# The end of a mixture-of-experts layer: expert 15's product ahead of expert 14's sums, parts taken straight from the accumulators, another split of the last LayerNorm

## Chip, core and metric

The kernel runs on one core of a Trainium2 chip. The metric is device microseconds of one execution. TensorE is written PE in the profile, VectorE DVE, ScalarE ACT, GpSimd POOL, SyncE SP; PSUM is the memory in which PE sums, SBUF the working memory.

## What is computed

One decoder layer on 512 tokens of width 1024. Only its last stage matters here: 16 experts, of which every token uses two, and a LayerNorm over the sum.

```python
for e in range(N_EXPERTS):                       # 16
    hidden = jax.nn.silu(hf @ w1[e]) * (hf @ w3[e])          # 1024 -> 512
    y = y + combine[:, e:e + 1] * (hidden @ w2[e])           # 512 -> 1024
...
h = layer_norm(DN_ALPHA * h + moe_out, ln3_g[l], ln3_b[l])
```

## The kernel before

Each expert has a block of 128 slots; its tokens are gathered into them from memory. `up(e)` makes the hidden rows, `turn_hidden(e)` transposes them on PE (four transposes, then one DVE copy, line L1453), `down(e)` makes the second product. Both products have a base part, which does slots 0 to 63 with matmuls 64 rows high, and a further part in `further`, which PE enters by a branch on the expert's token count: slots 64 to 95 if it has over 64 tokens, 96 to 127 if it has over 96. `down` sums the base part in the PSUM tile `a` (I-5387_acc in the rows; its two halves of partitions hold the two halves of the columns) and the further part in the PSUM tile `b` (I-5389_acc; four groups of 32 partitions, which hold the four quarters of the columns, with slots 64 to 95 in columns 0:256 and slots 96 to 127 in 256:512). There is one `a` and one `b` for all experts.

After `down(e)` ACT and DVE move the sums out and scale them by the tokens' gates: `a` in two ACT instructions of 64x512, `b` in four ACT and four DVE instructions of 32x256. For experts 0 to 13 the rows go to SBUF and a POOL DMA adds them into `yd` in memory, which already holds the residual. The program makes ACT and DVE wait for each other wherever both read the tile `b`, whichever partitions they read.

Experts 14 and 15 don't go through memory. Their scaled rows are split into a high part of 32-bit "r" type and a low rest (`split`, L191 on ACT and L192 on DVE), and for each of the four tiles of 128 tokens PE multiplies a 0/1 matrix `own[e]` by both parts (`combine`, L1535 and L1536: four matmuls of 128x512 per tile and expert). The tile's rows from `yd` are added either by PE with an identity (`from_memory`, L1557, tiles 0 and 2) or by DVE while it takes the sums (`totals`, L1573, tiles 1 and 3). The last LayerNorm then goes tile by tile: the sums (`sums_vector` for tile 0, `totals` and `mean` for the others), the squares on ACT (`deviation`, L1582) with two small POOL instructions behind them (L1583 and the power -1/2, L214), the centred rows times the gain on DVE (`centred`, L1589, L1592), and the scaling with the shift: on DVE (`shifted`, L1602), or on ACT with an addition on POOL (`scaled`, L1596 and L1597: tile 0 and half of tile 1). SP sends the rows out.

Each engine works through its own list in the order of the program; a semaphore lets an instruction wait for another engine. The order of the end is written out by hand:

```python
    h = up(NE - 1)
    r = last_loads()
    load_tiles(range(NT))
    parts(NE - 2, down(NE - 2), r)
    turn_hidden(NE - 1, h)
    begin_tile(0)                       # expert 14's part of tiles 0 and 1
    begin_tile(1)
    parts(NE - 1, down(NE - 1), 3)
```

Of the kernel before, what the change touches and what calls it, by code (L numbers as in the profile page):

```python
# [96 lines left out]
def tile_kernel(ctx, tc, x, mem, ln_in_g, ln_in_b, w_in, hg_lb_logits, hg_norm_g, w_branch_a, w_branch_b,  # L97
# [1357 lines left out]

    def down(e):
        x, (a, b) = hT.pop(e), sums_down
        ws = [W.get(j) for j in q_w2[e]]
        for k, w in enumerate(ws):
            for n in range(2):  # L1460
                nc.tensor.matmul(a[64 * n:64 * n + 64], x[:, k, 0:64], w[:, n * 512:(n + 1) * 512], start=k == 0,  # L1461
                                 stop=k == 3)
            tick()
# [12 lines left out]
        y = ys[e % 2]  # L1476
        for n in range(2):
            s = slice(64 * n, 64 * n + 64)
            nc.scalar.activation(y[0:64, n * 512:(n + 1) * 512], a[s], AF.Copy, scale=gates_at[s, 0, e:e + 1])  # L1479
        for i in range(4):  # L1480
            s, c = slice(32 * i, 32 * i + 32), slice(256 * i, 256 * i + 256)
            nc.scalar.activation(y[64:96, c], b[s, 0:256], AF.Copy, scale=gates_at[s, 1, e:e + 1])  # L1482
            nc.vector.tensor_scalar(y[96:128, c], b[s, 256:512], gates_at[s, 2, e:e + 1], None, op0=ALU.mult)  # L1483
# [42 lines left out]

    def parts(e, y, room):
        b = slot(room, [P, 2, 2, T], F32R, name=f"yg{e}")
        yh[e], yl[e] = b[:, 0], b[:, 1]
        for n in range(2):  # L1530
            split(yh[e][:, n], yl[e][:, n], y[:, n * T:(n + 1) * T])

    def combine(e, t, o, start, stop):
        for n in range(2):
            nc.tensor.matmul(o[n], own[e][:, t * P:(t + 1) * P], yh[e][:, n], start=start, stop=False)  # L1535
            nc.tensor.matmul(o[n], own[e][:, t * P:(t + 1) * P], yl[e][:, n], start=False, stop=stop)  # L1536

    def begin_tile(t):
        os[t] = [acc(), acc()] if t % 2 else [msp(), msp()]
        combine(NE - 2, t, os[t], True, False)  # L1540
# [53 lines left out]

    def scaled(t, h):
        nc.scalar.mul(ys[t][:, h], ys[t][:, h], st[:, t, 5:6])  # L1596
        nc.gpsimd.tensor_tensor(ys[t][:, h], ys[t][:, h], gs[1][:, h], op=ALU.add)  # L1597
        nc.sync.dma_start(out[t * P:(t + 1) * P, h], ys[t][:, h])

    def shifted(t, parts):  # L1600
# [4 lines left out]

    from_memory(0)
    combine(NE - 1, 0, os[0], False, True)
    combine(NE - 1, 1, os[1], False, True)
    begin_tile(2)
# [15 lines left out]
    totals(3)
    mean(3)
    scaled(1, halves[0])
    shifted(1, [halves[1]])
    deviation(3)
    shifted(2, [slice(0, D)])  # L1630
    centred(3)
    shifted(3, halves)

# [29 lines left out]
```

## Time and profile before

| | us |
|---|---|
| three runs | 910.92, 911.67, 914.58 (median 911.67) |
| the profiled execution | 912.46 |
| its span in the profile | 910.7 |
| PE busy in the span | 861.2 (95%) |
| DVE, ACT, POOL busy | 460.0, 335.2, 134.9 |

Times in the rows are counted from the start of the span. A row of the timeline has the start, the length, the engine, the line, the operation, out<-in, the shapes and the count of a run of like instructions; in brackets stands how long the engine stood idle before it and what ended that. PEclk in the windows is the granted clock of PE as a share: 1.00 is 2.4 GHz, 0.50 is 1.2 GHz.

### The profile page before, as it was taken

Reading aid. Unit: us, or ns where it says so; the run is one execution under the profiler, and the core shown is the slowest. Engines: PE = TensorE matmul, PEld = TensorE weight load, DVE = VectorE, ACT = ScalarE, POOL = GpSimd, SP = SyncE. Lnnn points to the kernel's source line nnn. Section 1 sums busy time; section 2 is a strip of 40 time slices with the busy share of each in tenths; the row PEclk is TensorE's granted clock in tenths of the full one; section 3 lists DMA queues with packets and bytes.
Section 4 is the critical chain, followed back from the end, with each engine's and each line's share of the span. In section 5 each row is a group of like instructions: output and inputs, shape, how many; then the busy total and the mean of one; then the engine's idle time right before and its main releaser. Section 6 shows DMA issues by size and latency. Waiting matters only on the chain. (4 is left out here: it accounts for less than half of the span.)

```text
span 910.7 us, 13810 instructions
## 1 busy us (share of the span) xinstructions
PE 861.2 (95%) x5356; PEld 592.5 (65%) x5356; DVE 460.0 (51%) x810; ACT 335.2 (37%) x633; POOL 134.9 (15%) x222
## 2 busy tenths in 40 slices
PE   6999999999999999999999999999999998899974
PEld 5888777888777778888888887863333332244432
DVE  6642576644666547579635666833332323222227
ACT  3332335643554554304524543222433232222133
POOL 5300000001212220015000001301121111111104
PEclk8999999999999999999999999999999999899996
DMA  8433323222212264315722686879999999999632
GB/s 293 154 111 93 94 71 94 70 61 89 71 58 70 70 220 168 99 47 155 219 93 72 230 296 211 299 272 370 382 344 349 353 351 328 359 350 359 255 131 93
DMA packets 63029, 177.67 MB, mean 195 GB/s; under 512 B 7813, under 2 KB 7845, under 8 KB 62944
## 3 DMA queue, kind: packets, MB, share of 16 engines
q1 hardware_dynamic: 54400, 154.16, 48.8%
q0 software_dynamic: 8400, 21.79, 7.6%
q8 instruction: 61, 1.00, 0.4%
q10 hardware_dynamic: 144, 0.52, 0.1%
q14 instruction: 24, 0.20, 0.1%
HBM read 168.47 MB, written 15.73 MB: 202 GB/s over the span
## 5 line engine op out<-in xcount | busy, mean ns | idle before, releaser
L1423 PE MATMUL I-5383_acc<-ring,xgT 128*64 128x512 f32 x284 | 78.7, 600 | 2.5 <-DMA ring<-in_moe_w_dram 2.5
L67 DVE TENSOR_TENSOR I-69_out<-raws,I-69_out 128x1024 fp32r<-128x1024 f32 x24 | 29.3, 1222 | 38.2 <-ACT I-69_out L65 37.9
L1423 PEld LDWEIGHTS I-5383_acc<-ring,xgT 128*64 128x64 f32 x284 | 23.4, 138 | 36.3 <-issue 31.3
L1483 DVE TENSOR_SCALAR ringgb<-I-5389_acc,wgb 32x256 f32<-32x256 f32 x32 | 15.5, 483 | 57.2 <-ACT ringgb L1482 57.2
L1483 DVE TENSOR_SCALAR wx<-I-5389_acc,wgb 32x256 f32<-32x256 f32 x32 | 15.5, 483 | 55.2 <-ACT wx L1482 55.2
L661 DVE TENSOR_TENSOR_SCAN wx<-sbk 128x128 f32<-128x128 f32 (+3 forms) x32 | 27.1, 847 | 28.7 <-POOL sbk L657 28.7
L65 ACT CAST I-73_out<-raws 128x1024 fp32r<-128x1024 f32 x23 | 24.1, 1050 | 45.5 <-PE I-3563_acc L188 17.1
L67 DVE TENSOR_TENSOR I-71_out<-raws,I-71_out 128x1024 fp32r<-128x1024 f32 x22 | 26.9, 1222 | 24.7 <-ACT I-71_out L65 24.6
L65 ACT CAST I-69_out<-raws 128x1024 fp32r<-128x1024 f32 x25 | 26.3, 1050 | 33.0 <-issue 9.2
L65 ACT CAST I-71_out<-raws 128x1024 fp32r<-128x1024 f32 x24 | 25.3, 1055 | 24.9 <-PE I-384_acc L187 4.6
L67 DVE TENSOR_TENSOR I-73_out<-raws,I-73_out 128x1024 fp32r<-128x1024 f32 x21 | 25.7, 1222 | 16.1 <-ACT I-73_out L65 15.8
L1423 PE MATMUL I-5383_acc<-raws,xgT 128*64 128x512 f32 x64 | 31.0, 618 | 0.5 <-DMA raws<-in_moe_w_dram 0.5
L657 POOL TENSOR_SCALAR_AFFINE_SELECT sbk<-sbk 128x128 f32<-128x128 f32 x32 | 14.3, 447 | 94.5 <-ACT sbk L652 50.2
L1161 POOL DMA_INDIRECT ringgb<-x2d,s x15 | 15.6, 1037 | 76.9 <-PE I-5689_ms L1396 9.3
L1434 PE MATMUL I-5385_acc<-ring,xgT 128*32 128x256 f32 x408 | 26.4, 380 | 0.0
L1479 ACT ACTIVATE ringgb<-I-5387_acc,wgb 64x512 f32<-64x512 f32 x16 | 10.9, 683 | 35.1 <-issue 19.7
L1434 PEld LDWEIGHTS I-5385_acc<-ring,xgT 128*32 128x32 f32 x408 | 14.1, 110 | 13.8 <-issue 4.9
L1479 ACT ACTIVATE wx<-I-5387_acc,wgb 64x512 f32<-64x512 f32 x16 | 10.9, 683 | 30.6 <-PE I-5387_acc L1461 17.0
L1273 POOL DMA_INDIRECT yd<-ringgb,s x7 | 11.2, 1602 | 68.4 <-DVE ringgb L1483 68.4
L214 POOL TENSOR_TENSOR I-1461hgss<-I-1461hgss,mhalf 128x4 f32<-128x4 f32 x1 | 1.0, 1047 | 136.9 <-DVE I-1461hgss L565 136.9
L1482 ACT ACTIVATE ringgb<-I-5389_acc,wgb 32x256 f32<-32x256 f32 x32 | 14.9, 464 | 17.1 <-DVE ringgb L1483 13.2
L1482 ACT ACTIVATE wx<-I-5389_acc,wgb 32x256 f32<-32x256 f32 x32 | 14.9, 464 | 16.6 <-DVE wx L1483 13.2
(3524 smaller groups left out, 2456.5 us busy)
## 6 DMA issues: line engine op xcount, KB each, us to landing
ring<-in_moe_w_dram SPq DMA_DIRECT2D x114, 512.0 KB, 12.5
raws<-in_w_in_dram SPq DMA_DIRECT2D x44, 512.0 KB, 3.7
ringout<-in_moe_w_dram SPq DMA_DIRECT2D x32, 512.0 KB, 13.2
raws<-in_moe_w_dram SPq DMA_DIRECT2D x20, 512.0 KB, 12.4
xres<-in_moe_w_dram SPq DMA_DIRECT2D x16, 512.0 KB, 13.2
raws<-in_xa_wk_dram SPq DMA_DIRECT2D x7, 512.0 KB, 3.8
raws<-in_xa_wv_dram SPq DMA_DIRECT2D x7, 512.0 KB, 4.6
raws<-in_w_mix_out_dram SPq DMA_DIRECT2D x6, 512.0 KB, 5.7
```

The lines of the kernel that those rows point to most:

```text
L65: self.nc.scalar.copy(hi, raw)
L67: eng.tensor_tensor(lo, raw, hi.bitcast(F32), op=ALU.subtract)
L214: nc.gpsimd.tensor_tensor(o, v, mhalf[:, :v.shape[-1]], op=ALU.pow)
L657: nc.gpsimd.affine_select(kp[:, d], kp[:, d], pattern=[[-1, P]], compare_op=ALU.is_gt, fill=1.0, base=w * (P - 1), channel_multiplier=1 - ...
L661: nc.vector.tensor_tensor_scan(rest[:, :n][:, ::-1], kp[:, n:0:-1], kp[:, n:0:-1], 1.0, ALU.mult, ALU.bypass)
L1161: nc.gpsimd.indirect_dma_start(out=gbr[:, 1], out_offset=None, in_=x2d[:, :], in_offset=bass.IndirectOffsetOnAxis(ap=gidx[:, e:e + 1], axi ...
L1273: nc.gpsimd.indirect_dma_start(out=yd[:, :], out_offset=bass.IndirectOffsetOnAxis(ap=idx, axis=0), in_=y, in_offset=None, bounds_check=T - ...
L1423: nc.tensor.matmul(a[64 * i:64 * i + 64], x[:, c, 0:64], w[:, k * 512:(k + 1) * 512], start=c == 0, stop=c == 7)
L1434: nc.tensor.matmul(b[32 * i:32 * i + 32, 256 * g:256 * g + 256], x[:, c, 64 + 32 * g:96 + 32 * g], ws[c // 2][i // 2][:, o:o + 256], start ...
L1479: nc.scalar.activation(y[0:64, n * 512:(n + 1) * 512], a[s], AF.Copy, scale=gates_at[s, 0, e:e + 1])
L1482: nc.scalar.activation(y[64:96, c], b[s, 0:256], AF.Copy, scale=gates_at[s, 1, e:e + 1])
L1483: nc.vector.tensor_scalar(y[96:128, c], b[s, 256:512], gates_at[s, 2, e:e + 1], None, op0=ALU.mult)
```

## The change

For experts 0 to 13 `to_rows` takes the same ten instructions in another order: on `b`, ACT does its four first (both sets of slots of quarters 0 and 1), then DVE its four (quarters 2 and 3).

For experts 14 and 15 no scaled rows are kept. `to_parts` makes both parts of each piece out of PSUM: ACT writes the high part, then DVE reads the same piece again, scales it and takes the high part off. A piece is 64x512 of `a` (two for each expert) or 32x256 of `b` (eight). Expert 14's transposes for 15 move ahead of its further part; expert 15's product comes ahead of every sum over expert 14, further part first; the whole combination of all four tiles stands behind it, tile by tile in the order 0, 1, 3, 2. Tile 1 gets its rows from `yd` by PE instead of DVE, and only tile 3 still by DVE. Both `scaled` calls are gone, so that DVE does all shifts.

```diff
     def down(e):
...
-        further(e, part)
-        for j in q_w2[e]:
-            W.done(j)
-        finish()
+        return base, lambda: further(e, part), done
...
+    def further_at(quarters):
+        for g in (1, 0):
+            for i in quarters:
+                yield (g + 1, slice(32 * i, 32 * i + 32), slice(256 * g, 256 * g + 256), sums_down[1],
+                       slice(64 + 32 * g, 96 + 32 * g), slice(256 * i, 256 * i + 256))
+
+    def to_rows(e):
         y = ys[e % 2]
...
+        for g, s, c, z, r, k in [*base_at(), *further_at((0, 1))]:
+            nc.scalar.activation(y[r, k], z[s, c], AF.Copy, scale=gates_at[s, g, e:e + 1])
+        for g, s, c, z, r, k in further_at((2, 3)):
+            nc.vector.tensor_scalar(y[r, k], z[s, c], gates_at[s, g, e:e + 1], None, op0=ALU.mult)
...
+    def to_parts(e, at):
+        for g, s, c, z, r, k in at:
+            nc.scalar.activation(yh[e][r, k], z[s, c], AF.Copy, scale=gates_at[s, g, e:e + 1])
+            nc.vector.scalar_tensor_tensor(yl[e][r, k], z[s, c], gate[r, e:e + 1], yh[e][r, k].bitcast(F32),
+                                           op0=ALU.mult, op1=ALU.subtract)
...
-    parts(NE - 2, down(NE - 2), r)
+    base, more_slots, done = down(NE - 2)
+    base()
     turn_hidden(NE - 1, h)
-    begin_tile(0)
-    begin_tile(1)
-    parts(NE - 1, down(NE - 1), 3)
+    more_slots()
+    done()
+    to_parts(NE - 2, base_at())
+    to_parts(NE - 2, further_at(range(4)))
+    base, more_slots, done = down(NE - 1)
+    more_slots()
+    base()
+    done()
+    to_parts(NE - 1, further_at(range(4)))
+    to_parts(NE - 1, base_at())
...
-            if t == 2:
+            if t < NT - 1:
                 nc.scalar.activation(zn, os[t][n], AF.Copy, accum_out=st[:, t, n:n + 1])
...
+    for t in (0, 1):
+        from_memory(t)
+        combine(NE - 2, t)
+        combine(NE - 1, t)
+    os[3] = [acc(), acc()]
+    combine(NE - 2, 3)
+    combine(NE - 1, 3)
     from_memory(2)
+    combine(NE - 2, 2)
+    combine(NE - 1, 2)
     sums_vector(0)
     centred(0)
-    scaled(0, slice(0, D))
-    totals(2)
     totals(1)
+    shifted(0, [slice(0, D)])
...
-    shifted(3, halves)
+    shifted(3, [slice(0, D)])
+    shifted(2, halves)
```

PE's list between the two products. Before (w2k are transposed hidden rows, yg the parts; L1451 are the transposes for expert 15, L1461 its base part):

```order
L1451 MATMUL I-8562_ms<-ident,I-8486w2k 128x128 x4
L1535 MATMUL I-8571_ms<-yg_8557,I-8493w2k 128x512
L1536 MATMUL I-8571_ms<-yg_8557,I-8493w2k 128x512
L1535 MATMUL I-8573_ms<-yg_8557,I-8493w2k 128x512
L1536 MATMUL I-8573_ms<-yg_8557,I-8493w2k 128x512
L1535 MATMUL I-8579_acc<-yg_8557,I-8493w2k 128x512
L1536 MATMUL I-8579_acc<-yg_8557,I-8493w2k 128x512
L1535 MATMUL I-8581_acc<-yg_8557,I-8493w2k 128x512
L1536 MATMUL I-8581_acc<-yg_8557,I-8493w2k 128x512
L1461 MATMUL I-5387_acc<-ring_4379,I-8568w2k 64x512 x2
```

Eight matmuls over expert 14's parts stand between the transposes and expert 15's product. In the changed kernel, the end of expert 14's product and the start of 15's, with the semaphores that an instruction waits for in brackets (L1472 is the further part; I-8392w2k belongs to expert 14, I-8521w2k to 15):

```order
L1472 MATMUL I-5389_acc<-ring_4376,I-8392w2k 32x256 x4
L1412 UNCONDITIONAL_BRANCH
L1412 UNCONDITIONAL_BRANCH [waits PE_49]
L1410 UNCONDITIONAL_BRANCH [waits PE_49]
L1410 COMPARE_AND_BRANCH
L1472 MATMUL I-5389_acc<-ring_4379,I-8521w2k 32x256 [waits DMAHW7_49,DVE_49]
L1472 MATMUL I-5389_acc<-ring_4379,I-8521w2k 32x256 x3
```

The transposes have moved up, between expert 14's base part and its further part, and no sum over its parts stands between the products any more. The first matmul of expert 15's further part, which writes `b`, waits for DVE: the value that it waits for is that of DVE's last reading of expert 14's `b`.

ACT's and DVE's lists for the two experts' sums. Before, DVE (ringgb holds expert 14's scaled rows, wx expert 15's):

```order
L1483 TENSOR_SCALAR ringgb<-I-5389_acc,wgb 32x256 [waits Activation_49] x3
L192 TENSOR_TENSOR yg_8557<-ringgb,yg_8557 128x512 [waits DMAHW0_49,DMAHW1_49,DVE_49,Activation_49]
L192 TENSOR_TENSOR yg_8557<-ringgb,yg_8557 128x512 [waits Activation_49]
L1453 COPY I-8568w2k<-I-8562_ms 128x512 [waits PE_49]
L1410 UNCONDITIONAL_BRANCH
```

And in the changed kernel, DVE (L1453 is the copy of expert 15's hidden rows; yg_8505 belongs to expert 14, yg_8506 to 15):

```order
L1453 COPY I-8521w2k<-I-8515_ms 128x512 [waits DVE_49,PE_49]
L1504 SCALAR_TENSOR_TENSOR yg_8505<-I-5387_acc,s_4905,yg_8505 64x512 [waits DMAHW1_49,DMAHW0_49,Activation_49]
L1504 SCALAR_TENSOR_TENSOR yg_8505<-I-5387_acc,s_4905,yg_8505 64x512 [waits Activation_49]
L1504 SCALAR_TENSOR_TENSOR yg_8505<-I-5389_acc,s_4905,yg_8505 32x256 [waits Activation_49] x8
L1410 UNCONDITIONAL_BRANCH
L1504 SCALAR_TENSOR_TENSOR yg_8506<-I-5389_acc,s_4905,yg_8506 32x256 [waits Activation_49] x8
L1504 SCALAR_TENSOR_TENSOR yg_8506<-I-5387_acc,s_4905,yg_8506 64x512 [waits Activation_49] x2
```

with ACT's list beside it:

```order
L1503 ACTIVATE yg_8505<-I-5389_acc,wgb 32x256 [waits PE_49]
L1503 ACTIVATE yg_8505<-I-5389_acc,wgb 32x256 [waits DVE_49] x7
L1410 UNCONDITIONAL_BRANCH
L1503 ACTIVATE yg_8506<-I-5389_acc,wgb 32x256 [waits DVE_49,PE_49]
L1503 ACTIVATE yg_8506<-I-5389_acc,wgb 32x256 [waits DVE_49] x7
L1503 ACTIVATE yg_8506<-I-5387_acc,wgb 64x512 [waits PE_49]
L1503 ACTIVATE yg_8506<-I-5387_acc,wgb 64x512 [waits DVE_49]
```

The copy of the hidden rows moved ahead of the sums. Four pieces of `b` per engine became eight, each DVE piece waits for its ACT piece and each ACT piece but the first for the DVE piece before it; the splits of whole rows are gone.

## Rows read from the trace of the kernel before

**Rows 1.** The chain of waits that ended last, its end, in order of time (start us, us, what; "issue" is time in which nothing shown was waited for, a q behind an engine is its queue).

```profile
876.37 3.58 PE I-5387_acc L1461 x16
879.95 3.64 PE I-5389_acc L1469 x64
...
883.61 0.47 ACT wx L1482
...
887.13 0.63 ACT yg L191
...
895.26 1.27 ACT ring L1571 x4
...
905.02 0.66 DVEq L1658
```

**Rows 2.** Busy time by stretch (from:to, length, busy time and instructions of each engine, granted clock, share of the 16 DMA engines, GB/s).

```profile
800.00:840.00 40.00, 37.85 (x364) 16.67 (x356) 9.37 (x16) 9.98 (x18) 5.27 (x4) 1.00 1.01 366
...
858.00:911.00 53.00, 33.26 (x264) 17.42 (x252) 24.63 (x39) 16.09 (x29) 13.12 (x17) 0.83 0.27 103
```

**Rows 3.** The timeline around expert 14's product and sums.

```profile
862.71 3.65 PE L1461 MATMUL I-5387_acc<-ring,I-8392w2k 128*64 128x512 f32 x16
...
866.30 1.93 PE L1469 MATMUL I-5389_acc<-ring,I-8392w2k 128*32 128x256 f32 x32
866.46 1.39 ACT L1479 ACTIVATE ringgb<-I-5387_acc,wgb 64x512 f32<-64x512 f32 x2 [3.00 <-PE I-5387_acc L1461]
868.39 0.46 ACT L1482 ACTIVATE ringgb<-I-5389_acc,wgb 32x256 f32<-32x256 f32 x1 [0.54 <-PEq L1412]
...
868.69 0.66 PE L1451 MATMUL I-8562_ms<-ident,I-8486w2k 128*128 128x128 f32 x4 [0.46 <-PEq L1412]
868.89 0.47 DVE L1483 TENSOR_SCALAR ringgb<-I-5389_acc,wgb 32x256 f32<-32x256 f32 x1 [3.79 <-ACT ringgb L1482]
...
869.89 0.48 DVE L1483 TENSOR_SCALAR ringgb<-I-5389_acc,wgb 32x256 f32<-32x256 f32 x1 [0.53 <-ACT ringgb L1482]
...
873.89 0.69 DVE L1453 COPY I-8568w2k<-I-8562_ms 128x512 f32<-128x512 f32 x1
...
876.30 1.08 PE L1461 MATMUL I-5387_acc<-ring,I-8568w2k 128*64 128x512 f32 x4
```

**Rows 4.** The timeline of the combination: the identity matmuls, tile 0's last matmul, two neighbours at the full clock, the last matmul of all.

```profile
883.47 1.13 PE L1557 MATMUL I-8571_ms<-ring,ident 128*128 128x512 f32 x2
...
884.43 1.02 PE L1557 MATMUL I-8573_ms<-ring,ident 128*128 128x512 f32 x2
...
889.13 0.50 PE L1536 MATMUL I-8573_ms<-yg,I-8496w2k 128*128 128x512 f32 x1
...
894.83 0.40 PE L1536 MATMUL I-8655_ms<-yg,I-8496w2k 128*128 128x512 f32 x1
...
895.06 0.40 PE L1535 MATMUL I-8657_ms<-yg,I-8496w2k 128*128 128x512 f32 x1
...
897.15 0.40 PE L1536 MATMUL I-8687_acc<-yg,I-8496w2k 128*128 128x512 f32 x1
```

**Rows 5.** Groups of like instructions after 860 us (line, engine, operation, out<-in, shapes, count, busy us, mean ns, idle time before them and its enders).

```profile
L1592 DVE SCALAR_TENSOR_TENSOR ring<-I-8571_ms,st,ring 128x512 f32<-128x512 f32 x1 | 0.8, 751 | 0.0
...
L1589 DVE SCALAR_TENSOR_TENSOR ring<-raws,st,ring 128x1024 f32<-128x1024 f32 x1 | 1.3, 1271 | 0.0
L1582 ACT ACTIVATE ring<-raws,st 128x1024 f32<-128x1024 f32 x1 | 1.1, 1148 | 0.1
```

**Rows 6.** Stretches with PE's granted clock at either level, columns as in rows 2.

```profile
10.25:15.50 5.25, 5.25 (x16) 4.07 (x17) 3.26 (x7) 4.13 (x6) 4.02 (x2) 0.50 1.05 409
781.20:787.00 5.80, 5.80 (x14) 1.70 (x15) 0.00 (x0) 0.00 (x0) 0.00 (x0) 0.50 0.98 355
868.95:872.40 3.45, 0.39 (x4) 0.15 (x2) 1.85 (x4) 1.88 (x4) 0.00 (x0) 1.00 1.03 420
872.59:875.80 3.21, 3.21 (x7) 2.28 (x8) 1.96 (x3) 0.48 (x1) 0.00 (x0) 0.50 0.14 57
889.70:892.80 3.10, 3.10 (x8) 2.35 (x8) 3.03 (x8) 0.62 (x1) 0.83 (x2) 0.50 0.00 0
```

and, from the timeline, a base part of another expert in the second of these stretches:

**Rows 7.** The timeline at 781 us.

```profile
781.20 6.58 PE L1461 MATMUL I-5387_acc<-ring,I-7510w2k 128*64 128x512 f32 x15 [3.07 <-issue]
```

**Rows 8.** The timeline of the LayerNorm's end: POOL's work and DVE's beside it.

```profile
893.40 2.36 POOL L1597 TENSOR_TENSOR ring<-ring,ring 128x1024 f32<-128x1024 f32 x1 [1.75 <-ACT ring L1596]
893.60 3.26 DVE L1589 SCALAR_TENSOR_TENSOR ring<-ring,st,ring 128x1024 f32<-128x1024 f32 x1
...
899.07 0.19 POOL L1583 TENSOR_SCALAR st<-st 128x1 f32<-128x1 f32 x1
899.34 0.55 POOL L214 TENSOR_TENSOR st<-st,mhalf 128x1 f32<-128x1 f32 x1
...
901.64 1.05 POOL L1583 TENSOR_SCALAR st<-st 128x1 f32<-128x1 f32 x1
902.56 1.27 DVE L1589 SCALAR_TENSOR_TENSOR ring<-raws,st,ring 128x1024 f32<-128x1024 f32 x1
902.77 1.47 POOL L214 TENSOR_TENSOR st<-st,mhalf 128x1 f32<-128x1 f32 x1
904.27 1.41 DVE L1602 SCALAR_TENSOR_TENSOR ring<-ring,st,ring 128x512 f32<-128x512 f32 x2 [0.44 <-POOL st L214]
```

More of the change, by code (lines that the diff above doesn't have):

```diff
@@ L1458, in down, with base @@
         ws = [W.get(j) for j in q_w2[e]]
[L1459 to L1463, printed above, removed]
+        def base():
+            for k, w in enumerate(ws):
+                for n in range(2):
+                    nc.tensor.matmul(a[64 * n:64 * n + 64], x[:, k, 0:64], w[:, n * 512:(n + 1) * 512], start=k == 0,
+                                     stop=k == 3)
+                tick()
         def part(g):
@@ L1470, in part, with done, base_at @@
                                      w[:, 256 * i:256 * i + 256], start=k == 0, stop=k == 3)
-        further(e, part)
-        for j in q_w2[e]:
-            W.done(j)
-        finish()
-        y = ys[e % 2]
[L1477 to L1483, printed above, removed]
-        return y
+        def done():
+            for j in q_w2[e]:
+                W.done(j)
+        return base, lambda: further(e, part), done
+    def base_at():
+        for n in range(2):
+            yield 0, slice(64 * n, 64 * n + 64), slice(0, 512), sums_down[0], slice(0, 64), slice(512 * n, 512 * n + 512)
+    def further_at(quarters):
[4 more added lines that the diff above has]
+    def to_rows(e):
+        y = ys[e % 2]
+        for g, s, c, z, r, k in [*base_at(), *further_at((0, 1))]:
+            nc.scalar.activation(y[r, k], z[s, c], AF.Copy, scale=gates_at[s, g, e:e + 1])
+        for g, s, c, z, r, k in further_at((2, 3)):
+            nc.vector.tensor_scalar(y[r, k], z[s, c], gates_at[s, g, e:e + 1], None, op0=ALU.mult)
+        return y
+    def to_parts(e, at):
[3 more added lines that the diff above has]
+                                           op0=ALU.mult, op1=ALU.subtract)
     for e in range(NE - 1):
@@ L1497, in tile_kernel @@
         if e > 0:
-            scatter(down(e - 1), gidx[:, e - 1:e])
+            for step in down(e - 1):
+                step()
+            finish()
+            scatter(to_rows(e - 1), gidx[:, e - 1:e])
         turn_hidden(e, h)
@@ L1525, in load_tiles, with combine, from_memory @@
             nc.gpsimd.dma_start(zs[t], yd[t * P:(t + 1) * P])
[L1527 to L1540, printed above, removed]
+    def combine(e, t):
+        for n, o in enumerate(os[t]):
+            for y in (yh[e], yl[e]):
+                nc.tensor.matmul(o, own[e][:, t * P:(t + 1) * P], y[:, n * T:(n + 1) * T], start=not begun[t, n],
+                                 stop=e == NE - 1 and y is yl[e])
+                begun[t, n] = True
+    def from_memory(t):
+        for n, o in enumerate(os[t]):
+            nc.tensor.matmul(o, ident, zs[t][:, n * T:(n + 1) * T], start=not begun[t, n], stop=False)
+            begun[t, n] = True
+    begun = dict.fromkeys(((t, n) for t in range(NT) for n in range(2)), False)
     h = up(NE - 1)
@@ L1544, in tile_kernel @@
     load_tiles(range(NT))
-    parts(NE - 2, down(NE - 2), r)
-    turn_hidden(NE - 1, h)
-    begin_tile(0)
-    begin_tile(1)
-    parts(NE - 1, down(NE - 1), 3)
+    for e, room in ((NE - 2, r), (NE - 1, 3)):
+        b = slot(room, [P, 2, D], F32R, name=f"yg{e}")
+        yh[e], yl[e] = b[:, 0], b[:, 1]
+    base, more_slots, done = down(NE - 2)
+    base()
+    turn_hidden(NE - 1, h)
+    more_slots()
[8 more added lines that the diff above has]
+    to_parts(NE - 1, base_at())
+    for t in range(NT - 1):
+        os[t] = [acc(), acc()] if t % 2 else [msp(), msp()]
     st = pp.tile([P, NT, 8], F32, name="st3")
@@ L1553, in tile_kernel @@
     halves = [slice(n * T, (n + 1) * T) for n in range(2)]
-    def from_memory(t):
-        for n in range(2):
-            nc.tensor.matmul(os[t][n], ident, zs[t][:, halves[n]], start=False, stop=False)
     def sums_vector(t):
@@ L1593, in centred @@
                                                op0=op, op1=ALU.mult)
[L1595 to L1598, printed above, removed]
     def shifted(t, parts):
@@ L1604, in shifted @@
             nc.sync.dma_start(out[t * P:(t + 1) * P, h], ys[t][:, h])
[L1606 to L1609, printed above, removed]
+    for t in (0, 1):
[5 more added lines that the diff above has]
+    combine(NE - 1, 3)
     from_memory(2)
-    combine(NE - 1, 2, os[2], False, True)
+    combine(NE - 2, 2)
+    combine(NE - 1, 2)
     sums_vector(0)
     centred(0)
-    scaled(0, slice(0, D))
-    totals(2)
     totals(1)
-    begin_tile(3)
-    combine(NE - 1, 3, os[3], False, True)
+    shifted(0, [slice(0, D)])
     mean(1)
@@ L1621, in tile_kernel @@
     centred(1)
+    totals(3)
+    mean(3)
+    deviation(3)
+    shifted(1, [slice(0, D)])
+    centred(3)
+    totals(2)
     mean(2)
@@ L1624, in tile_kernel @@
     centred(2)
[L1625 to L1631, printed above, removed]
-    shifted(3, halves)
+    shifted(3, [slice(0, D)])
+    shifted(2, halves)
 _INS = ['x', 'mem', 'ln_in_g', 'ln_in_b', 'w_in', 'hg_lb_logits', 'hg_norm_g', 'w_branch_a', 'w_branch_b',
```

## The prediction

> **What bounds the kernel now.** I read the busy time by stretch first. Up to 840 us the DMA engines are filled (share 1.01, 366 GB/s) and PE is busy in 37.9 of 40 us; after 858 us the share is 0.27 and PE works 33 of 53 us [rows 2]. So experts 0 to 13 are paced by the weights' transfers and PE behind them, and the end by a chain from engine to engine. Whatever only reorders ACT and DVE inside the first part is hidden; the end is not.
>
> The chain of waits names the pieces of the end: expert 15's product on PE, then ACT and DVE in turn over its sums, the split, the combination on PE, and the LayerNorm [rows 1]. I measure it by five points, read from the timeline: expert 15's product starts at 876.30; ACT takes its sums from 883.61; tile 0's last matmul starts at 889.13; PE's last matmul ends at 897.55; the span ends at 910.7 [rows 1, 3, 4]. What starts expert 15's product so late is not PE's own work: the transposes were over at 869.35, but their copy stands on DVE behind expert 14's sums and split (873.89), and eight matmuls over expert 14's parts stand ahead of the product on PE [rows 3].
>
> Two more things bear on the change. ACT and DVE alternate strictly on tile `b`: DVE's pieces start at 868.89 and 869.89, and each is idle while the other works [rows 3]. So a pair of pieces costs 1.00 us. And PE's clock falls when PE has idled: it stood at 0.50 from 872.59 to 875.80 after the idle time before it, and again from 889.70 to 892.80 [rows 6].
>
> **The change, stage by stage.** All sums are made against the profiled span of 910.7; that execution took 912.46, the median of the runs is 911.67, and the difference is added to the median.
>
> *Up to expert 15's product.* Removed: the two splits on ACT and DVE and eight matmuls. Added: the same sums in twice as many pieces, and the wait of the product's first matmul for DVE's last reading of `b`. Base part over at 866.3 [rows 3]. The transposes follow at once, 0.66; DVE copies by 867.7 (0.69). ACT has base piece 0 by 867.15 (1.39 for two). DVE's base piece: no such instruction is in the trace; the nearest, a scalar-tensor-tensor out of PSUM, takes 0.75 [rows 5], so 868.45; ACT's piece 1 to 869.2, DVE's to 869.95. PE's further part ends at about 869.1 (1.93 after the transposes), so `b` is ready. DVE's 32x256 piece: nearest 0.48 [rows 3]; bounds 0.47 and 0.75, and I take 0.48, the same shape out of the same tile. First piece to 870.45, seven more pairs of 1.00: 877.45. The product starts at 877.5, later by 1.2. Behind its first matmul on PE wait the base part, tile 0's identity matmuls and every sum of the combination.
>
> *Product to evacuation.* The further part comes first, and `b` is free for ACT as soon as it is done: 3.66 (879.95 to 883.61 [rows 1]) in place of 7.31. ACT starts at 881.2: a gain of 3.65 in the stage. The base part's 3.58 lie beside the evacuation of `b`.
>
> *Evacuation to tile 0.* Before: four pairs and the split, 883.61 to 889.13, 5.5. Now eight pairs, 8.0; ACT's first base piece starts after its eighth piece of `b`, at 888.7, and ends at 889.4; then DVE 0.75, ACT 0.69, DVE 0.75 with hand-overs of 0.03: 891.75. The last matmul of tile 0 starts at 891.8: 10.6, a loss of 5.1. This is the dearest term. The split took 2.0, 887.13 to 889.13 [rows 1, 4]; making the parts in the pieces costs four more pairs in `b` and puts `a`, whose ACT work used to be hidden ahead of `b`, at the end.
>
> *Combination.* Behind tile 0 stood 20 matmuls over parts and two of an identity; now 24 and four, because tile 1's share of expert 14 is no longer done early and tile 1 takes its rows from `yd` by PE. At the full clock a matmul costs 0.23 (894.83 to 895.06) and each identity matmul 0.96 (883.47 to 884.43) [rows 4]: 24 x 0.23 + 4 x 0.96 = 9.3, and the last one ends 0.4 later: 901.5. 9.7 in place of 8.4 (which holds a stretch at the low clock): a loss of 1.3.
>
> *LayerNorm's end.* Before, from PE's end 13.15. Now tile 2 is last: ACT's second copy with its sum ends 0.85 later (two such copies took 895.26 to 896.53 [rows 1], and the second can only start behind PE's last matmul); the mean, behind DVE's backlog, ends at 1.5; the squares 1.15 + 0.2; two POOL instructions; two half shifts 1.41; and 5.0 from DVE's end at 905.68 to the span's end, which stays (last transfer a half tile as before). POOL's two take 0.19 + 0.55 where DVE reads PSUM or nothing, but 1.05 and 1.47 beside DVE's whole-tile passes [rows 8]; two such passes stand on DVE at that time, so I take 1.05 + 0.55 with 0.1 of hand-over. Sum: 1.5 + 1.35 + 1.7 + 1.45 + 5.0 = 11.05 with the hand-overs. A gain of 2.1; the bounds are 10.2 (POOL undisturbed) and 12.0 (both delayed).
>
> The Trainium skill, page "SBUF — State Buffer", section "Who interferes with whom", says that a DVE instruction with two SBUF inputs and a GpSimd instruction that reads SBUF lock each other out for a whole instruction. The trace agrees: a DVE pass of 1.27 took 3.26 beside POOL's addition [rows 8]. By that rule alone the end would gain about 2 for each addition gone; most of it lies beside other waits, so the sum keeps 2.1 for both.
>
> *At nothing:* the new order for experts 0 to 13. Eight pieces back to back, four of 0.46 and four of 0.48, end 0.2 earlier than four pairs; the scatter behind them is hidden under the weights' transfers [rows 2] and `b` is not written again until the next expert. If that cover were gone, 14 x 0.2 = 2.8 either way. The copies to SBUF of other outputs and SP's five transfers in place of six lie beside DVE's work.
>
> Sum at the full clock: +1.2 - 3.65 + 5.1 + 1.3 - 2.1 = +1.9.
>
> **The clock.** Before, PE idled for 3.2 us after the transposes. Now it has nothing from 869.1 to 877.5, so it starts expert 15's product at the low clock. How long it stays there is bounded by the rows: 3.2 us where the clock fell as PE resumed (872.59), 5.3 and 5.8 where it had fallen before PE resumed (10.25, 781.20) [rows 6]. There matmuls take twice as long: a base part of 15 matmuls took 6.58 against 3.65 for 16 [rows 3, 7]. The new case is like the last two; I take 5.2, half of it lost: +2.6 (bounds 1.6, and 3.65 if the whole further part runs low). A second fall is likely while PE waits for `b` and `a` of expert 15 with only tile 0's matmuls to do; the same place had one before, 3.1 [rows 6]. It costs half, +1.65 with its edges (bounds 0 and 2.9). The 8.4 above already holds such a loss; the 9.7 does not.
>
> +1.9 + 2.6 + 1.65 = +6.15: span 916.85, and 911.67 + 6.15 = 917.8.
>
> **Rivals.**
>
> *The clock costs little.* PE is found at 2.4 GHz or recovers within a microsecond or two, in one or both places: +1.9 to +4.5, 913.6 to 916.2. For it: after 868.95 the clock stayed up for 3.4 us of almost no work [rows 6]. Against: 8.4 us of no work is longer than any idle time here that left it up. 0.18.
>
> *The pairs overlap* (the other side). If ACT could begin the next piece while DVE reads the last one, a pair would cost 0.5. The product would start at 874.0, the evacuation at 877.7; DVE would be through at 884.4, and with the same later stages and clock losses the end comes 7.35 earlier: span 909.5, 910.4, no slower than before; with the clock up too, 906. It decides from a pair of about 0.58 down. For it: the pieces lie on different partitions. Against: the program lists a wait for DVE at seven of ACT's eight pieces, and the old pieces, on different partitions too, alternated [rows 3]. 0.06.
>
> The Trainium skill, page "PSUM — Partial Sum Buffer", section "PSUM bank collisions raise a hardware error", says that two engines may use one bank at the same time if they touch different groups of 32 partitions. By that rule alone the pieces of different quarters could overlap and the time would be this rival's. No row shows such an overlap; the waits come from the program.
>
> *Both low stretches are long.* The whole further part and 5.8 us of the combination at 1.2 GHz: +1.9 + 3.65 + 2.9 = +8.45, 920.1 or more. 0.06.
>
> *POOL stays in the way.* Without additions POOL still reads SBUF four times; if both small instructions are delayed at the end, +1.0 on the forecast. Inside the range.
>
> **How the numbers follow.** Forecast 0.70: both falls, +4.6 to +8.4. Three runs of the same kernel spread over 0.4%, so 0.5% (4.6 us) is about what a measurement can tell from no change. Slower by more than that: nearly all of the forecast's cases and the long stretches, 0.70. Within 0.5%: the clock rival, most of the overlap, the forecast's lower edge, 0.26. Faster by more than 0.5%: the overlap with the clock up, 0.04. The range reaches from the sum without clock losses, 913.5, to both long stretches with a late POOL, 920.5.
>
> **What the profile after would show.** Right: eight pairs of 1.0 us on `b` for each expert; no PE work from about 869 to 877.5; the product's further part at 0.50 for most of its length, some 6 us instead of 3.7; tile 0's last matmul at about 894.5 to 896; DVE's whole-tile passes all at 1.27; some 11 us from PE's last matmul to the end. Wrong: pairs much shorter or longer than 1.0, a product that starts before 876 or runs at 1.00, DVE instead of PE setting the end after tile 0 (its own work there is six passes of 1.27, eight half-tile ones of about 0.7 and some small ones, 14.4 in all, which with the last 5.0 would end 1 us earlier than PE's chain at the full clock), or a change before 858 us, which no term here explains.

## The result, and the profile after

The changed kernel takes 918.4 us (median of 4 runs, 917.33 to 919.86) against 911.29 us for the kernel before (4 runs): a ratio of 1.0074, with a 95% interval from 1.0048 to 1.0100. It is slower by 7.1 us (by the interval, 4.4 to 9.1); 917.8 was predicted, as a change of +6.15. That the time agrees better than the change owes 0.4 us to the median of the kernel before, which was 911.67 when the prediction was made. The profiled execution took 917.33, its span 915.6.

The five points of the prediction can be read again in the timeline of the changed kernel; I count them from the start of expert 14's base part, because everything up to there began 2.23 us earlier in this execution (860.48 against 862.71 in [rows 3]). The timeline of the changed kernel at these points (L1464 is a base part, L1472 a further part, L1503 and L1504 the pieces on ACT and DVE, L1554 a matmul of the combination):

```profile
860.48 3.65 PE L1464 MATMUL I-5387_acc<-ring,I-8392w2k 128*64 128x512 f32 x16
...
867.63 0.48 DVE L1504 SCALAR_TENSOR_TENSOR yg<-I-5389_acc,s,yg 32x256 fp32r<-32x256 f32 x1
868.14 0.46 ACT L1503 ACTIVATE yg<-I-5389_acc,wgb 32x256 fp32r<-32x256 f32 x1 [0.84 <-DVE yg L1504]
868.64 0.48 DVE L1504 SCALAR_TENSOR_TENSOR yg<-I-5389_acc,s,yg 32x256 fp32r<-32x256 f32 x1 [0.53 <-ACT yg L1503]
...
875.28 1.08 PE L1472 MATMUL I-5389_acc<-ring,I-8521w2k 128*32 128x256 f32 x8 [8.70 <-DVE yg L1504]
...
881.81 0.46 ACT L1503 ACTIVATE yg<-I-5389_acc,wgb 32x256 fp32r<-32x256 f32 x1 [7.11 <-PE I-5389_acc L1472]
...
891.62 0.75 DVE L1504 SCALAR_TENSOR_TENSOR yg<-I-5387_acc,s,yg 64x512 fp32r<-64x512 f32 x1 [0.75 <-ACT yg L1503]
...
892.42 0.29 PEld L1554 LDWEIGHTS I-8642_ms<-yg,I-8496w2k 128*128 128x128 f32 x1 [0.50 <-DVE yg L1504]
...
904.02 0.63 PE L1554 MATMUL I-8650_ms<-yg,I-8496w2k 128*128 128x512 f32 x2
```

The reader sees DVE start a piece of `b` every 1.01 us, with ACT's piece in each gap, and PE idle for 8.70 us until the last of them frees the bank. The last matmul of tile 0 follows the weight load at 892.42, which waits for DVE's last piece; PE's last matmul ends at 904.65. Stage by stage, in us:

| stage | before | predicted | after | difference to before |
|---|---|---|---|---|
| expert 14's base part to expert 15's product | 13.59 | 14.8 | 14.80 | +1.21 |
| product to ACT's first piece of it | 7.31 | 6.26 | 6.53 | -0.78 |
| to tile 0's last matmul | 5.52 | 10.6 | 10.61 | +5.09 |
| to PE's end | 8.42 | 11.35 | 12.23 | +3.81 |
| to the span's end | 13.15 | 11.05 | 10.95 | -2.20 |
| sum | 47.99 | 54.1 | 55.12 | +7.13 |

The stages add up to the 7.1 us of the medians; the earlier start lies outside them (experiment 6). They come from one execution of each kernel, so an agreement to the tenth is in part luck. The windows of the changed kernel, columns as in [rows 2]:

```profile
866.60:870.85 4.25, 0.00 (x0) 0.00 (x0) 2.37 (x5) 2.07 (x5) 0.00 (x0) 0.99 1.00 405
870.95:875.20 4.25, 0.00 (x0) 0.00 (x0) 2.12 (x5) 1.86 (x4) 0.00 (x0) 0.50 0.05 21
875.30:881.00 5.70, 5.70 (x56) 2.71 (x60) 0.00 (x0) 0.00 (x0) 0.00 (x0) 0.50 0.00 0
881.20:888.10 6.90, 6.90 (x36) 2.54 (x28) 2.89 (x6) 2.99 (x7) 0.00 (x0) 1.00 0.01 2
888.20:890.10 1.90, 0.00 (x0) 0.00 (x0) 0.97 (x2) 1.31 (x3) 0.00 (x0) 1.00 0.00 0
891.70:897.95 6.25, 6.25 (x10) 3.31 (x11) 4.97 (x7) 0.00 (x0) 0.82 (x2) 0.50 0.02 7
```

The granted clock was 0.50 (1.2 GHz) from 870.95, with PE idle since 866.6, to 881.0, although PE was busy through the last 5.7 us of that; and again from 891.7 to 897.95, a stretch that holds only 10 matmul instructions. These windows lie inside the low stretches. Followed in steps of a quarter of a microsecond, the two stretches of the kernel before last 3.4 us each, the two of the changed kernel 10.2 (870.8 to 881.0) and 6.8 (891.2 to 898.1).

The chain of waits that ended last leaves PE before PE's end:

```profile
898.27 0.48 PE I-8644_acc L1554 x2
...
898.77 0.60 ACT ring L1602
...
904.53 1.16 ACT ring L1602 x4
```

From tile 1's sums on (898.77) ACT and DVE set the pace, up to ACT's copies of tile 2 (L1602). The second of these starts at 905.01, behind the first and 0.36 us after PE's last matmul. So PE's end is only a mark between the last two stages; together they took 23.18 us, where 22.4 were predicted.

At the end the two halves of the LayerNorm's change can be seen side by side in the timeline (L1628 is a whole-tile pass on DVE, L1614 and L214 the two small operations on POOL):

```profile
907.16 1.28 DVE L1628 SCALAR_TENSOR_TENSOR ring<-ring,st,ring 128x1024 f32<-128x1024 f32 x1
907.29 1.20 POOL L1614 TENSOR_SCALAR st<-st 128x1 f32<-128x1 f32 x1 [1.02 <-ACT ring L1613]
908.58 0.55 POOL L214 TENSOR_TENSOR st<-st,mhalf 128x1 f32<-128x1 f32 x1
909.16 1.42 DVE L1628 SCALAR_TENSOR_TENSOR ring<-ring,st,ring 128x512 f32<-128x512 f32 x2 [0.71 <-POOL st L214]
```

DVE's pass takes 1.28, not the 3.26 it took beside POOL's addition [rows 8], while POOL's operation on one column takes 1.20 instead of 0.19: it ends 0.05 us after DVE's pass. The Trainium skill, page "SBUF — State Buffer", section "Who interferes with whom", says that a DVE instruction with two SBUF inputs and a GpSimd instruction that reads SBUF lock each other out for a whole instruction; these rows agree.

### The profile page after: what moved, and what is told of

It is laid out like the page before. It is cut to its first block, busy times and chain, and to the rows that moved or that the text cites. A ratio compares the mean times of both kernels' runs of the same rounds, so it can differ in the third digit from the quotient of the medians.

```text
span 915.6 us, 13843 instructions
## 1 busy us (share of the span) xinstructions
PE 863.4 (94%) x5360; PEld 593.1 (65%) x5360; DVE 462.7 (51%) x815; ACT 335.9 (37%) x639; POOL 130.4 (14%) x220
## 5 line engine op out<-in xcount | busy, mean ns | idle before, releaser
L1498 DVE TENSOR_SCALAR ringgb<-I-5389_acc,wgb 32x256 f32<-32x256 f32 x28 | 13.6, 487 | 48.5 <-ACT ringgb L1496 47.8
L1498 DVE TENSOR_SCALAR wx<-I-5389_acc,wgb 32x256 f32<-32x256 f32 x28 | 13.6, 487 | 43.9 <-ACT wx L1496 43.2
L1273 POOL DMA_INDIRECT yd<-wx,s x7 | 11.2, 1595 | 68.7 <-DVE I-8392w2k L1453 16.8
L1496 ACT ACTIVATE ringgb<-I-5387_acc,wgb 64x512 f32<-64x512 f32 x14 | 9.6, 683 | 30.2 <-issue 16.4
L214 POOL TENSOR_TENSOR I-1461hgss<-I-1461hgss,mhalf 128x4 f32<-128x4 f32 x1 | 1.0, 1047 | 136.0 <-DVE I-1461hgss L565 136.0
L1496 ACT ACTIVATE wx<-I-5387_acc,wgb 64x512 f32<-64x512 f32 x14 | 9.6, 683 | 23.7 <-PE I-5387_acc L1464 10.1
L1423 PE MATMUL I-5383_acc<-ringout,xgT 128*64 128x512 f32 x80 | 17.9, 595 | 0.0
```

The costliest lines, as they stand in the source:

```text
L1273: nc.gpsimd.indirect_dma_start(out=yd[:, :], out_offset=bass.IndirectOffsetOnAxis(ap=idx, axis=0), in_=y, in_offset=None, bounds_check=T - ...
L1423: nc.tensor.matmul(a[64 * i:64 * i + 64], x[:, c, 0:64], w[:, k * 512:(k + 1) * 512], start=c == 0, stop=c == 7)
L1496: nc.scalar.activation(y[r, k], z[s, c], AF.Copy, scale=gates_at[s, g, e:e + 1])
L1498: nc.vector.tensor_scalar(y[r, k], z[s, c], gates_at[s, g, e:e + 1], None, op0=ALU.mult)
```

## The experiments

The theory: the loss is the making of the parts in eight pairs of 1.0 us on one bank, paid twice, and the two falls of the clock that PE's waits bring; the LayerNorm's end is a gain. The rivals: the order of the products is what costs; the clock costs little; the pairs would overlap anyway. Each kernel was timed beside the kernel before, whose median was 911.02 us in 33 runs beside experiments 1 to 4 and 910.82 us in 25 runs beside 5 to 8. Since the span before expert 14's base part varies from execution to execution, I also give the length from there to the span's end in the profiled execution: 47.99 before, 55.12 after.

**1. The parts from rows again.** In the changed kernel the lines that make the parts from PSUM are replaced, for both experts, by rows and a split:

```diff
-    to_parts(NE - 1, further_at(range(4)))
-    to_parts(NE - 1, base_at())
+    rows_and_parts(NE - 1)
...
+    def rows_and_parts(e):
+        y = to_rows(e)
+        for n in range(2):
+            split(yh[e][:, n * T:(n + 1) * T], yl[e][:, n * T:(n + 1) * T], y[:, n * T:(n + 1) * T])
```

> The changed kernel with one part undone: experts 14 and 15 are evacuated to rows again and the rows split into the two parts from SBUF, as in the kernel before; the order of the products and of the last LayerNorm stay as changed. Theory (the eight pairs of 1.0 us on one bank are the loss): expert 15's product starts about 10.5 us after expert 14's base part instead of 14.8, and the stage from its evacuation to tile 0's last matmul takes about 5.5 us instead of 10.6; with the clock's second fall unsure that is 9 to 12 us, a time of 906 to 910 us, below both kernels. Rival (the order of the products is the loss, whatever way the parts are made): 917 to 919 us.

Measured: 910.21 us, ratio 0.9989 (0.9973 to 1.0004). The timeline of this kernel (L1496 and L1498 are the rows on ACT and DVE, L191 and L192 the split):

```profile
861.44 3.65 PE L1464 MATMUL I-5387_acc<-ring,I-8392w2k 128*64 128x512 f32 x16
...
867.76 1.93 ACT L1496 ACTIVATE ringgb<-I-5389_acc,wgb 32x256 f32<-32x256 f32 x4 [1.17 <-issue]
869.72 1.99 DVE L1498 TENSOR_SCALAR ringgb<-I-5389_acc,wgb 32x256 f32<-32x256 f32 x4 [3.31 <-ACT ringgb L1496]
...
871.81 0.64 PE L1472 MATMUL I-5389_acc<-ring,I-8521w2k 128*32 128x256 f32 x8 [4.26 <-DVE ringgb L1498]
...
880.79 1.38 ACT L1496 ACTIVATE wx<-I-5387_acc,wgb 64x512 f32<-64x512 f32 x2 [8.43 <-PE I-5387_acc L1464]
```

Rows empty the bank in 4.0 us (four pieces of ACT, four of DVE) where parts need 8: the product starts 10.4 us after the base part, as expected, and the median is 8.2 us below the changed kernel's. In the profiled execution, the third longest of the twelve, base part to end is 49.56: 5.6 below the changed kernel, but 1.6 above the kernel before. So the parts from PSUM cost 5.6 to 8.2 us, most of the loss or all of it. What the order of the products costs by itself is then between nothing, by the medians, and 1.8 us, by this execution against that of experiment 2; these runs do not settle it. The time lies just above the 906 to 910 that I expected and is not shown to be below the kernel before. The trace has two things that I had not counted: the rows take the base pieces first, so ACT waits until 880.79 for a base part that the new order puts last; and the clock fell twice here too, from 872.6 to 876.0 and from 886.2 to 893.1.

**2. The new end alone.** The kernel before with the changed kernel's `totals`, without `scaled`, with the new order of the LayerNorm, and with tile 1's rows of `yd` added by PE:

```diff
-            if t == 2:
+            if t < NT - 1:
                 nc.scalar.activation(zn, os[t][n], AF.Copy, accum_out=st[:, t, n:n + 1])
...
+    from_memory(1)
     combine(NE - 1, 1, os[1], False, True)
```

> The kernel before with the last LayerNorm alone changed: no additions on GpSimd, tile 1 with the identity's matmuls and ScalarE's totals, tile 3 ahead of tile 2. Theory (the new end is worth 2.1 us, and the identity's two matmuls of tile 1 cost PE about 1.9 us of it): the stretch from PE's last matmul to the span's end is 11.0 us instead of 13.15, the combination 1.9 us longer, the time 910.5 to 911.5 us, no change. Rival (the new end is worth more than it costs wherever it stands): 909.2 us or less. Rival (the small operations on GpSimd in the way eat the gain): 912 us or more.

Measured: 910.15 us, ratio 0.9983 (0.9966 to 1.0000), no difference that this measurement can tell; base part to end 47.75. PE's last matmul in this kernel's timeline:

```profile
887.33 0.50 PE L1536 MATMUL I-8573_ms<-yg,I-8496w2k 128*128 128x512 f32 x1
...
897.19 0.40 PE L1536 MATMUL I-8671_ms<-yg,I-8496w2k 128*128 128x512 f32 x1
```

From there to the span's end of 908.4 are 10.8 us (13.15 before), and from tile 0's last matmul to PE's end 10.26 (8.42 before): 2.35 gained and 1.84 given back, about what the two identity matmuls of tile 1 take. The first theory holds in both terms (2.1 and 1.9 expected), though the time lies 0.35 us under its range.

**3. PE kept busy.** The changed kernel with matmuls into a tile of PSUM that nobody reads:

```diff
+    def fill(n):
+        p = msp()
+        for i in range(n):
+            nc.tensor.matmul(p, ident, h, start=True, stop=True)
+    fill(8)
     base, more_slots, done = down(NE - 1)
...
     to_parts(NE - 1, base_at())
+    fill(7)
```

> The changed kernel with idle PE kept busy: 8 matmuls of 128x128 by 128x512 into a PSUM tile that nobody reads stand ahead of expert 15's product, and 7 ahead of tile 0's sums; nothing else differs. Theory (the granted clock falls because PE waits, and that costs time twice): both stretches stay at 1.00, the further part of expert 15 takes 3.6 us instead of 6.5 and the combination about 9.7 instead of 12.1, the time is about 913 us (912 to 915). Rival (the clock costs little, since the work waits for the evacuation anyway): 917 to 919 us. If the clock falls in spite of the matmuls, the two stretches stay as they are and the time too.

Measured: 914.78 us, ratio 1.0035 (1.0021 to 1.0049): 3.6 us less than the changed kernel, with nothing removed (base part to end 51.82). The windows and two entries of the chain of waits of this kernel:

```profile
867.80:874.90 7.10, 7.06 (x16) 2.96 (x16) 3.87 (x8) 3.10 (x7) 0.00 (x0) 1.00 0.56 226
876.10:902.10 26.00, 26.00 (x138) 13.89 (x138) 13.90 (x25) 9.03 (x19) 1.57 (x4) 1.00 0.05 21
```

```profile
876.09 3.66 PE I-5389_acc L1472 x64
...
883.33 6.21 PE I-8650_ms L1566 x14
```

The clock stays at 1.00 in both places, and the further part takes 3.66 instead of 6.51. The second filling stands on the chain itself: DVE's last piece ended at 890.38, and tile 0's sums, behind the filling, only at 893.1. So it hides what it gained.

**4. Two banks.** The changed kernel with the second group of further slots summed in a bank that is free by then, and the pieces taken from the two banks in turn:

```diff
-                    nc.tensor.matmul(b[32 * i:32 * i + 32, 256 * g:256 * g + 256], x[:, 2 * g + k % 2, s],
+                    nc.tensor.matmul(b[g][32 * i:32 * i + 32, 256 * g:256 * g + 256], x[:, 2 * g + k % 2, s],
...
+        b = [b, sums_up[1] if e > NE - 3 else b]
...
+        last = len(quarters) == 4
+        for g, i in [(g, i) for i in quarters for g in (1, 0)] if last else [(g, i) for g in (1, 0) for i in quarters]:
+            yield (..., sums_up[1] if last and g else sums_down[1], ...)
```

> The changed kernel with the two further sums of experts 14 and 15 in a bank each, and the pieces taken from the two in turn, so that ScalarE and VectorE never need the same bank at one time. Theory (a pair takes 1.0 us only because the two engines wait for each other on one bank): eight pairs take about 4.3 us instead of 8.1, twice; 7.6 us less, and 2.9 more if the shorter wait keeps the clock up: 908 to 911 us. Rival (the two engines slow each other at PSUM, or the pair is bound by the one's result that the other needs): 916 to 919 us.

Measured: 907.37 us, ratio 0.9955 (0.9938 to 0.9972): 11 us below the changed kernel, a little more than expected, and faster than the kernel before (base part to end 44.23). Its timeline (I-5385 and I-5389 are the two banks) and windows:

```profile
861.87 3.65 PE L1465 MATMUL I-5387_acc<-ring,I-8392w2k 128*64 128x512 f32 x16
...
870.04 0.48 DVE L1505 SCALAR_TENSOR_TENSOR yg<-I-5385_acc,s,yg 32x256 fp32r<-32x256 f32 x1
870.05 0.46 ACT L1504 ACTIVATE yg<-I-5389_acc,wgb 32x256 fp32r<-32x256 f32 x1
870.56 0.48 DVE L1505 SCALAR_TENSOR_TENSOR yg<-I-5389_acc,s,yg 32x256 fp32r<-32x256 f32 x1
870.56 0.46 ACT L1504 ACTIVATE yg<-I-5385_acc,wgb 32x256 fp32r<-32x256 f32 x1
...
873.22 1.08 PE L1473 MATMUL I-5389_acc<-ring,I-8521w2k 128*32 128x256 f32 x8 [5.24 <-DVE yg L1505]
```

```profile
873.10:876.60 3.50, 3.38 (x36) 1.91 (x40) 0.01 (x1) 0.00 (x0) 0.00 (x0) 0.52 0.02 7
876.80:894.90 18.10, 18.07 (x92) 9.94 (x84) 13.73 (x25) 8.86 (x19) 1.57 (x4) 1.00 0.08 30
```

A pair costs 0.51 us, and each engine's piece lasts what it lasted alone, 0.46 and 0.48: reading at the same time from two banks slows neither. The product starts 11.35 us after the base part instead of 14.80. The clock fell once still, for 3.5 us, but not a second time: from 876.8 on PE never waits.

**5. Banks of its own for expert 15.** As 4, and expert 15's product goes to banks that expert 14's evacuation does not hold (the tiles of the output are allotted their banks in another order to suit):

```diff
+        if e == NE - 1:
+            a, b = sums_up[0], [msp(), msp()]
```

> The kernel with two banks and, further, banks of its own for expert 15's product (the one of the gated sums and two of the small pool), so that PE need not wait for expert 14's evacuation. Theory (what is left of PE's wait, 5.2 us ahead of the product, is the wait for the bank alone): the product starts about 6 us after expert 14's base part instead of 11.4, PE is busy through, the clock stays at 1.00, and the sums wait only for the last piece of expert 15, which VectorE ends about 18 us after that base part; PE ends at about 28 us instead of 33: 901 to 904 us. Rival (the evacuation of both experts by ScalarE and VectorE is the bound by now and the last LayerNorm waits behind it): 905 to 908 us.

Measured: 901.61 us, ratio 0.9891 (0.9876 to 0.9906): 9.2 us faster than the kernel before and 5.8 faster than experiment 4 (base part to end 38.35). Its timeline:

```profile
861.85 3.65 PE L1470 MATMUL I-5387_acc<-ring,I-8392w2k 128*64 128x512 f32 x16
...
868.64 0.64 PE L1478 MATMUL I-8578_ms<-ring,I-8521w2k 128*32 128x256 f32 x8 [0.69 <-PEq L1412]
...
879.73 0.50 PE L1563 MATMUL I-8626_ms<-yg,I-8496w2k 128*128 128x512 f32 x1 [0.29 <-DVE yg L1513]
...
888.62 0.63 PE L1563 MATMUL I-8658_ms<-yg,I-8496w2k 128*128 128x512 f32 x2
```

The product starts 6.8 us after the start of the base part and PE ends 27.4 us after it (44.2 in the changed kernel); PE waits for the parts only once more, 0.29 us. The wait for the bank was the rest of PE's wait; the clock stays at 1.00 throughout, as the windows of this kernel show:

```profile
868.60:879.40 10.80, 10.76 (x91) 5.44 (x91) 9.33 (x19) 8.43 (x18) 0.00 (x0) 1.00 0.36 147
879.80:889.00 9.20, 9.20 (x33) 6.06 (x33) 8.22 (x15) 3.73 (x8) 1.57 (x4) 1.00 0.15 58
```

**6. The loop's edit alone.** The kernel before with the new order of the row pieces. The lines stand in `down`, which all sixteen experts use, so the edit reaches the rows of experts 14 and 15 too, and not only those of the loop:

```diff
-            nc.scalar.activation(y[64:96, c], b[s, 0:256], AF.Copy, scale=gates_at[s, 1, e:e + 1])
-            nc.vector.tensor_scalar(y[96:128, c], b[s, 256:512], gates_at[s, 2, e:e + 1], None, op0=ALU.mult)
+            if i < 2:
+                nc.scalar.activation(y[r, c], z, AF.Copy, scale=by)
+            else:
+                nc.vector.tensor_scalar(y[r, c], z, by, None, op0=ALU.mult)
```

> The kernel before with one edit of the change: in the loop over the experts ScalarE evacuates the base part and quarters 0 and 1 of the further part, VectorE quarters 2 and 3, in the changed order. Theory (the DMA sets the pace there, so the edit is worth nothing): 910 to 912 us, no change. Rival (the changed trace's earlier start of the end, 2.2 us, comes from this edit): about 909 us.

Measured: 910.26 us, ratio 0.9994 (0.9982 to 1.0007): nothing that this measurement can tell, as the prediction had it for the loop (base part to end 47.85). The start of expert 14's base part, in this kernel's timeline and in that of experiment 7, which has the same loop:

```profile
859.55 3.65 PE L1461 MATMUL I-5387_acc<-ring,I-8392w2k 128*64 128x512 f32 x16
```

```profile
864.50 3.65 PE L1464 MATMUL I-5387_acc<-ring,I-8392w2k 128*64 128x512 f32 x16
```

With one and the same loop these two starts lie 4.95 us apart. The earlier start of the changed kernel's profiled execution, 2.23, lies within that, and the median shows no gain of this size from the edit.

This run shows one thing more. In its profiled execution the clock did not fall a second time:

```profile
885.60:893.00 7.40, 7.40 (x27) 4.86 (x27) 7.23 (x12) 3.37 (x7) 3.23 (x3) 1.00 0.00 1
```

From tile 0's last matmul to PE's end it took 6.89 us, where the kernel before took 8.42 with its fall; but from that matmul to the span's end it took 21.21 against 21.57. DVE was busy in 7.23 of these 7.40 us, and the chain of waits of this execution runs over DVE there. So in the kernel before, whose DVE has the same work at this place, the second fall can have cost little at the end.

**7. The base part first.** In the changed kernel, for expert 15:

```diff
+    base()
     more_slots()
-    base()
     done()
+    to_parts(NE - 1, base_at())
     to_parts(NE - 1, further_at(range(4)))
-    to_parts(NE - 1, base_at())
```

> The changed kernel with expert 15's base part run and evacuated ahead of its further part. Theory (the further part waits for the last piece of expert 14's bank in either order; the base part, whose bank is free earlier, fits under that wait): the base part starts about 7 us after expert 14's and is done under the pairs, its own two pairs no longer stand behind the eight of the further part, the further part starts where it did; about 1.7 us less, 915.5 to 917.5 us, or up to 3 less again if the work under the wait keeps the clock up. Rival (the order chosen, further part first, is the better one, since its evacuation covers the base part): 918.4 us or more.

Measured: 914.45 us, ratio 1.0028 (1.0015 to 1.0040), 4 us below the changed kernel, as expected for a clock that stays up longer (base part to end 51.1). Its timeline and two windows:

```profile
871.68 1.08 PE L1464 MATMUL I-5387_acc<-ring,I-8521w2k 128*64 128x512 f32 x4 [1.07 <-DVE yg L1504]
...
879.31 0.64 PE L1472 MATMUL I-5389_acc<-ring,I-8521w2k 128*32 128x256 f32 x8 [3.98 <-DVE yg L1504]
```

```profile
880.70:883.60 2.90, 2.90 (x32) 1.50 (x28) 0.75 (x1) 0.23 (x1) 0.00 (x0) 0.50 0.03 6
890.90:897.70 6.80, 6.08 (x10) 3.05 (x11) 5.26 (x8) 0.85 (x2) 0.83 (x2) 0.52 0.00 1
```

The further part starts 14.81 us after expert 14's base part, as late as in the changed kernel, so putting it first bought nothing: it waits for the bank in either order. Under that wait PE does the base part, its idle time is 3.98 instead of 8.70, and the first low stretch shrinks from 10.2 to 3.4 us (880.4 to 883.8). The rival falls.

**8. The first filling alone.** As 3, without the second filling.

> The changed kernel with matmuls into an unread PSUM tile ahead of expert 15's product alone (8 of 128x128 by 128x512), and none ahead of tile 0's sums. Theory (the first fall of the clock costs the further part 2.9 us, the second, which stays, the rest): the further part takes 3.6 us, the combination stays near 12 us, the time is about 915.5 us (914.8 to 916.5). Rival (the first fall is hidden by the evacuation that follows): 918 us.

Measured: 914.61 us, ratio 1.0035 (1.0020 to 1.0050), base part to end 51.32: 3.8 us less than the changed kernel, a little better than expected and equal to experiment 3. Its windows:

```profile
877.50:881.00 3.50, 3.50 (x64) 1.96 (x64) 0.00 (x0) 0.00 (x0) 0.00 (x0) 1.00 0.02 5
892.10:895.40 3.30, 3.30 (x6) 1.38 (x5) 3.14 (x6) 0.00 (x0) 0.82 (x2) 0.50 0.01 2
```

Of the 3.8 us, 2.9 are the further part at the full clock (3.66 for 6.51). The other 0.9 come from the second low stretch, which lasted 3.4 us here and 6.8 in the changed kernel, with the same work. Why it was shorter, the rows do not show.

## Why the prediction was right, and where it was off

*The eight pairs.* Both stages that rest on them came out to 0.02 us: the product at 14.80 (14.8), the stage to tile 0's last matmul 10.61 (10.6). DVE's unknown base piece took 0.75, the value taken, its small piece 0.48. Experiments 1 and 4 show that this is the cause and not only the place: without the pairs most of the loss or all of it is gone, and with pairs of 0.51 all of it.

*The rival on the other side.* The pairs did not overlap, because on one bank the program makes the engines wait for each other. Experiment 4 is that rival made true with two banks, and its 907.4 lies inside the rival's 906 to 910.4. The Trainium skill, page "PSUM — Partial Sum Buffer", section "PSUM bank collisions raise a hardware error", would allow it in one bank too, on different groups of 32 partitions; that was not tried, since it means taking away the program's waits.

*Further part first.* The gain of 3.65 in the second stage stood in the sum, but the stage before was compared with a product that starts with the base part. Experiment 7 shows that the base part could have gone under the wait at no cost. The arithmetic of the sum was right (-3.65 + 2.6 against -0.78 measured); to read it as a gain of the order would be wrong.

*The first fall of the clock.* Predicted 2.6 within 1.6 and 3.65; the stage shows 6.53 - 3.66 = 2.9, and experiments 3 and 8 give these 2.9 back.

*The second fall.* This is the term that was mis-sized: 1.65, taken from a stretch of 3.1 us in [rows 6]. It lasted 6.8, of which 5.6 lie behind tile 0's last matmul. The combination's stage took 12.23; at the full clock I had 9.7, and experiment 3 shows 9.4 (892.66 to 902.11). So the fall cost 2.5 to 2.8, close to the upper bound of 2.9. It explains 0.9 of the 1.0 us by which the sum was short; 0.3 more from the first fall and 0.1 less at the end make up the rest, within rounding. By these sums the two falls cost 5.4 to 5.7 us; without them the stages would stand at +1.5 to +1.7, near the +1.9 at the full clock. That is worked out and not measured: experiment 3 removes both falls but pays for the second with its filling. The kernel before keeps its own two falls in this comparison, and by experiment 6 the second of them can have cost it little.

*The LayerNorm's end.* 10.95 against 11.05, with POOL's operation at 1.20 and 0.55 (1.05 and 0.55 assumed). Experiment 2 adds that this gain and tile 1's identity matmuls nearly cancel, which the prediction had in two different stages (-2.1 here, 2 x 0.96 in the combination).

*What sets the end after tile 0.* The prediction had PE's chain there, with DVE's own work 1 us shorter at the full clock, and named DVE in its place as a sign of being wrong. That sign came in part: PE leads only to tile 1's sums, then ACT and DVE. The forecast did not suffer, because the two chains lie close together (0.36 us at PE's end) and both start behind the low stretch.

*The range.* Its upper end, 920.5, is less than its own terms give (920.1 with 1.0 for a late POOL is 921.1). The result lies far from it.

*At nothing.* Experiment 6 agrees.

*Still open:* what sets the length of the second low stretch. It was 3.4 us in the kernel before and in experiments 2 and 8, 6.8 in the changed kernel and in experiments 1 and 7. It did not come in experiments 3 to 5, where PE had no long wait ahead of it, nor in experiment 6, where PE waited 0.75 and 1.61 us. Open too is what the order of the products costs by itself (experiment 1).

## What to carry to other kernels

When two engines empty one PSUM bank piece by piece, look in the trace whether their pieces alternate; if they do, the program takes turns on the bank, and spreading the sums over two banks can halve the time, as here (1.01 to 0.51 us a pair), with the same pieces. When PE waits for a bank to be emptied, give the next product a bank that is free already: here that was worth 5.8 us on top of the two banks, while the new orders of experiments 2 and 6 were worth nothing that could be measured. A wait of PE on the critical chain can be dearer than its length, because the matmuls behind it may run at the low clock: here the wait of 8.7 us added 2.9 to the further part. Put work that is due anyway under it; experiment 7 did so and gained 4 us. And ask what else is late: where DVE is nearly as late as PE, a low clock costs little (experiment 6).

## What the runs showed of the hardware

Eight matmuls whose result nobody reads made the kernel 3.8 us faster; what changed behind them was the granted clock, which stayed at 1.00 for the further part and was low for 3.4 us instead of 6.8 later. The low clock outlasted the idle time by far: in the changed kernel PE was busy without a gap for 5.7 us (875.30 to 881.00) before the clock was granted again. And ACT and DVE can read PSUM at the same time from two banks with no loss that the rows show (0.46 and 0.48 us a piece, alone or together).
